# Two-layer mLSTM and RG-LRU trunk on one core: sums of weight blocks held back and spread over the layer, and block products placed away from the gates

## The chip, the cores and the metric

The kernel runs on one core of a Trainium2 chip. The metric is device time in microseconds of one execution. Before the change the median of three runs is 1538.05 us (1536.64 to 1540.25). This kernel's engines are TensorE (PE, matmuls), VectorE (DVE), ScalarE (ACT), GpSimd (POOL) and SyncE (SP). SP and POOL mostly issue DMAs here, and each engine, and each DMA-issuing queue, works its instructions off in their order.

## The reference

`x` has 256 tokens of 2048 columns, all float32. Two layers of the same kind follow each other, then a last RMS norm:

```python
def hybrid_layer(x, norm_g, w_in, ...):
    u = rms_norm(x, norm_g)
    p = u @ w_in
    qk, v, o, z_a, ig, fg, xb, z_b = jnp.split(p, SPLIT_AT, axis=-1)
    qk = jax.nn.silu(causal_dwconv(qk, qk_conv))
    ...
    h = mlstm_chunkwise(q, k, v, i_pre, log_f)
    h = h * jax.nn.sigmoid(o)
    ...                                  # head norm
    y_a = h * jax.nn.silu(z_a)
    xc = causal_dwconv(xb, lru_conv_w) + lru_conv_b
    y_b = rg_lru(xc, w_a, b_a, w_x, b_x, lam) * jax.nn.silu(z_b)
    return x + jnp.concatenate([y_a, y_b], axis=-1) @ w_out
```

`w_in` is 2048 x 12304 and `w_out` 4096 x 2048, so each layer reads some 134 MB of weights for 256 tokens. `rg_lru` has two gates, each a block-diagonal product of `xc` with a 256 x 256 block per head and a sigmoid, and then a linear recurrence over the tokens.

## The kernel before

**Tiles and stages.** A layer is worked in four groups g of 512 columns (two heads). For each group there are "in" items (o, qk, v, z, xb, zb: 512 columns of `w_in`), one "gate" item (the two gates' blocks), and for the group before four "out" items (512 columns of `w_out` each, added to x in DRAM). An item is cut into units of 1 MB of weights, a unit into two halves of 512 KB. All weights are float32 and are split for the matmuls: `prepare` copies a half to wH in a rounded format on ScalarE (L336) and subtracts it on VectorE to get wL (L186, the line of the helper `tt_`). A half of an "in" item is then twelve matmuls of 512 columns (L360): activations' high part by wH and wL, low part by wH, for two row tiles of tokens.

**The loop.** The order of halves is a list, `order_`. For each half the loop loads ahead on SP (three `raw` tiles), prepares up to three halves ahead (`AHEAD = 3`, four buffers of wH and wL), runs the matmuls, runs what follows the item (`after`), and then calls `pump`, which steps background generators by a budget. The generators do everything else: the convolutions of qk and xb, the attention, the gates' functions, the sums below. A scheduler then orders the instructions of each engine by what it expects to be ready; `order(a, b)` adds an edge that keeps a behind b on an engine, without a wait.

**Block products.** Two items of each layer, z of group 2 and o of group 3 (`PAIR`), aren't computed as such. Together they are a 2 x 2 product of blocks (tokens by input rows, input rows by the two items), and the kernel uses seven block products in place of eight. For that it needs sums of blocks:

- Sums of activations, `block_sums`: S1 to S4, made on VectorE (`sum_t`, `sums`; L186) and ScalarE (L987) from `x_s`, in pieces of 128x512.
- Sums of weights, `weight_sums`: a start transfer copies half a unit from the weights to a DRAM tile `w_d` (L1026, issued by SP), and accumulating transfers add further ones (L1028, issued by POOL). For each layer that is 8 starts and 16 accumulations of 512 KB each. The last eight accumulations wait until the products 5 and 6 have loaded what they overwrite.
- The products, `block_halves`: fourteen pairs of halves for each layer, a pair being 1 MB and only twelve matmuls (L1091 to L1093, into `ps_b`). They load from the weights or from `w_d` (L296) and are laid evenly into `order_` between the first v item and the place of z of group 2. The last one calls `z_post`.

**Other names.** `gates_gen` computes the input and forget gates (`scs`); their result goes by DMA to `nG_d` and back, broadcast, to `nb` (both on POOL's queue), from which VectorE makes `E` (L194). `swapped` transposes an evacuated item: VectorE's `blk`, four DMAs on SP to `moved` in DRAM, one back on POOL's queue to `fr`. `xcs` (L186) is the split of the convolved xb, `xc`; the gate's matmuls (L792, `ps_gt`) read it, and ScalarE's sigmoids, exponentials and square roots (L797 to L828) follow. `z_post` computes `sz` on ScalarE and `za` on VectorE and starts the product with the attention's result.

Of the kernel before, what the change touches and what calls it, by code (L numbers as in the profile page):

```python
# [9 lines left out]
F32 = mybir.dt.float32  # L10
# [19 lines left out]
BORDER = 7  # L30
BLANKS = 7


# [59 lines left out]
def tile_trunk(ctx, tc, x, xt, par, gw, gb, ws, final_g, out):  # L93
# [189 lines left out]
    def load_unit(hf):  # L283
# [4 lines left out]
        if n < 4:  # L288
            w = 512 if n == 0 else 1024
            u = blocks[item, j]  # L290
            for o in range(0, 2048, w):
                if o % 1024 == 0:
                    load_xt(n, o // 1024)
                nc.sync.dma_start(out=raw[:, o : o + w], in_=ws[u][:, o : o + w])
        elif item is None:
            nc.sync.dma_start(out=raw, in_=hf["from"])  # L296
            if "loaded" in hf:
                st[hf["loaded"]] = True
        elif hf["paired"]:
            o = 1024 * (j % 2)  # L300
            for s_ in range(2):
                u = blocks[item, 2 * s_ + j // 2]
                nc.sync.dma_start(out=raw[:, 1024 * s_ : 1024 * s_ + 1024], in_=ws[u][:, o : o + 1024])
        else:
            nc.sync.dma_start(out=raw, in_=ws[blocks[item, j]])
        if 3 <= n < 7:
# [164 lines left out]
    def swapped(tok, blk=None, back=G):  # L471
# [7 lines left out]
        for a in range(4):  # L479
            nc.sync.dma_start(out=moved[:, a].rearrange("(m j) n -> j m n", m=4), in_=blk[32 * a : 32 * a + 32])  # L480
        back.dma_start(out=fr.rearrange("p a c t i -> p a (c t i)"), in_=moved)
        return fr
# [434 lines left out]
    def out_chunk(l, g, c):  # L917
# [54 lines left out]
    def block_sums(l):  # L972
# [3 lines left out]
        def part(r, c, a, k):  # L976
            return x_.bitcast(F32)[:, 8 * c + k : 8 * c + k + 4, a, P * r : P * r + P]

        def made(i, key, terms):
            to = sums[i]  # L980
            for k in (0, 4):
                ks = slice(k, k + 4)
                two = [work.tile([P, 4, P], F32, tag=tag, name="sum_t") for tag in ("tok", "blk")]
                for a in range(2):
                    terms(two, a, k, ks)
                tt_(two[0], two[0], two[1], ALU.add)
                S.copy(out=to[:, 0, ks], in_=two[0])  # L987
                tt_(to[:, 1, ks], two[0], to.bitcast(F32)[:, 0, ks], ALU.subtract)
                yield 2.6
            st[key, l] = True  # L990

        def s1(two, a, k, ks):
            tt_(two[a], part(1, 1, a, k), part(1, 0, a, k), ALU.subtract)

        def s2(two, a, k, ks):
            stt(two[a], sums[0].bitcast(F32)[:, a, ks], -1.0, part(0, 0, a, k), ALU.mult, ALU.subtract)

        def s3(two, a, k, ks):
            tt_(two[a], part(0, 0, a, k), part(1, 0, a, k), ALU.subtract)

        def s4(two, a, k, ks):
            tt_(two[a], sums[0].bitcast(F32)[:, a, ks], part(0, 0, a, k), ALU.add)
# [13 lines left out]

    def weight_sums(l):


        def moved(to, start, r, c):  # L1020
# [11 lines left out]
        yield from moved(0, True, 0, 0)  # L1032
        yield from moved(0, False, 0, 1)
        yield from moved(1, True, 1, 1)
        yield from moved(1, False, 0, 1)
        while ("loaded", l, 5) not in st:
            yield "wait"
        yield from moved(0, False, 1, 1)
        while ("loaded", l, 6) not in st:
            yield "wait"  # L1040
        yield from moved(0, False, 1, 0)

    def block_halves(l):
# [28 lines left out]
        def end4():  # L1072
# [8 lines left out]
            bg.append(gen())  # L1081
            z_post(l, PAIR[0][1], st["res", l])

# [338 lines left out]
```

## Time and profile before

| What | Value |
|---|---|
| Runs, median (lowest to highest) | 1538.05 us (1536.64 to 1540.25) |
| Profiled execution: its time | 1541.39 us |
| Profiled execution: its span | 1539.7 us |
| PE busy | 1490.2 us, 97% |
| DVE busy | 1138.8 us, 74% |
| ACT busy | 964.4 us, 63% |
| HBM over the span | 265 GB/s |
| Mean granted TensorE clock | 0.986 |

The profile is of one execution. Group rows name line, engine, operation and tiles, then count, busy time, mean duration in ns, idle time of the engine just ahead and who ended it. A half's twelve matmuls overlap, so a row's mean duration (392 ns) isn't the time that a further one costs; that is read from how many run in a full window. A row of windows gives a stretch, its length, the five engines' busy time, the granted clock, the DMA engines' mean busy share and GB/s. Layer 0 runs until about 745 us and layer 1 from there.

### The profile page before, as it was taken

How to read it: one execution, taken by the hardware profiler on the slowest of the kernel's cores; microseconds unless marked ns; L12 is line 12 of the kernel's file. 1: busy time of each engine (PE TensorE's matmuls, PEld its weight loads, DVE VectorE, ACT ScalarE, POOL GpSimd, SP SyncE). 2: the span in 40 equal slices, each digit the busy share in tenths (PEclk: the TensorE clock that was granted, in tenths of full speed). 3: DMA queues.
4: the chain of work that ended last, by engine and by line, in shares of the span. 5: the costliest groups of instructions: out<-in, count | busy, mean ns of one | idle time of the engine just before them, and what ended most of it. 6: DMA issues, size and time to landing. Idle time of an engine off the chain costs nothing.

```text
span 1539.7 us, 18745 instructions
## 1 busy us (share of the span) xinstructions
PE 1490.2 (97%) x6782; PEld 1232.9 (80%) x6782; DVE 1138.8 (74%) x1562; ACT 964.4 (63%) x1242; POOL 112.5 (7%) x186
## 2 busy tenths in 40 slices
PE   9978879999999999999999999999999999999997
PEld 7857758888788888888888877888888888888886
DVE  5777766767776787676975999865896578767785
ACT  6545656556655685657675568655675567755675
POOL 0050100000000000000000000000000000000002
PEclk9999889999999999999999999999999999999999
DMA  9999968886977776876696575787778687678773
GB/s 337 305 266 326 276 213 250 244 266 221 286 246 253 243 225 234 254 263 221 229 334 210 190 271 170 260 241 247 264 253 280 228 256 235 239 227 265 246 261 122
DMA packets 100014, 383.44 MB, mean 249 GB/s; under 512 B 10944, under 2 KB 31440, under 8 KB 76880
## 3 DMA queue, kind: packets, MB, share of 16 engines
q1 hardware_dynamic: 83504, 327.41, 60.8%
q0 software_dynamic: 13952, 50.35, 15.6%
q10 hardware_dynamic: 2464, 4.47, 0.8%
q8 instruction: 53, 0.87, 0.2%
q14 instruction: 41, 0.34, 0.1%
HBM read 344.95 MB, written 62.41 MB: 265 GB/s over the span
## 4 chain that ended last, share of the span: by engine, by line
PE 74%; DMA 10%; DVE 5%; issue 5%; ACT 5%; SPq 1%; POOL 0%; ACTq 0%; POOLq 0%; DVEq 0%
PE acc L360 62%; DMA raw<-in_ws_dram 6%; DVE wL L186 2%; PE ps_gt L792 2%; ACT wH L336 2%; DMA moved<-blk 2%; PE acc L373 1%; DMA fr<-moved 1%; PE ps_b L1092 1%; PE ps_b L1093 1%; PE ps_b L1091 1%; DMA nb<-nG_d 1%; DVE xc L189 1%; DMA nG_d<-scs 1%; PE acc L1187 1%
## 5 line engine op out<-in xcount | busy, mean ns | idle before, releaser
L360 PE MATMUL acc<-wH,x_s 128*128 128x512 f32 x2752 | 862.0, 392 | 13.3 <-ACT wH L336 13.2
L186 DVE TENSOR_TENSOR wL<-raw,wH 128x1024 fp32r<-128x1024 f32 (+1 forms) x556 | 663.4, 1202 | 284.5 <-ACT wH L336 282.6
L336 ACT CAST wH<-raw 128x1024 fp32r<-128x1024 f32 (+1 forms) x556 | 570.2, 1037 | 390.7 <-PE acc L360 277.7
L360 PEld LDWEIGHTS acc<-wH,x_s 128*128 128x128 f32 x2752 | 520.7, 189 | 124.5 <-ACT wH L336 16.7
L360 PE MATMUL acc<-wL,x_s 128*128 128x512 f32 x1376 | 540.3, 394 | 17.3 <-DVE wL L186 17.2
L360 PEld LDWEIGHTS acc<-wL,x_s 128*128 128x128 f32 x1376 | 260.6, 189 | 78.1 <-DVE wL L186 24.4
L360 PE MATMUL acc<-wH,yaH 128*128 128x512 f32 x224 | 87.5, 391 | 0.0
L360 PE MATMUL acc<-wH,yaL 128*128 128x512 f32 x224 | 87.3, 390 | 0.0
L360 PE MATMUL acc<-wH,ybL 128*128 128x512 f32 x224 | 87.3, 390 | 0.0
L360 PE MATMUL acc<-wH,ybH 128*128 128x512 f32 x224 | 87.2, 389 | 0.0
L360 PE MATMUL acc<-wL,ybH 128*128 128x512 f32 x224 | 87.2, 389 | 0.0
L360 PE MATMUL acc<-wL,yaH 128*128 128x512 f32 x224 | 87.2, 389 | 0.0
L792 PE MATMUL ps_gt<-xcs,wH 128*128 128x256 f32 x256 | 47.3, 284 | 5.4 <-ACT gate L797 5.4
L477 DVE STREAM_TRANSPOSE blk<-tok 128x1024 f32<-128x1024 f32 x33 | 40.9, 1239 | 15.0 <-ACT tok L467 14.8
L360 PEld LDWEIGHTS acc<-wH,ybL 128*128 128x128 f32 x224 | 42.1, 188 | 9.1 <-DVE ybL L186 0.3
L360 PEld LDWEIGHTS acc<-wH,yaL 128*128 128x128 f32 x224 | 42.0, 188 | 8.9
L360 PEld LDWEIGHTS acc<-wL,ybH 128*128 128x128 f32 x224 | 42.1, 188 | 8.5
L360 PEld LDWEIGHTS acc<-wH,ybH 128*128 128x128 f32 x224 | 42.0, 188 | 8.6
L360 PEld LDWEIGHTS acc<-wH,yaH 128*128 128x128 f32 x224 | 42.1, 188 | 8.4
L360 PEld LDWEIGHTS acc<-wL,yaH 128*128 128x128 f32 x224 | 42.1, 188 | 8.2
L467 ACT ACTIVATE tok<-acc,rstd 128x512 f32<-128x512 f32 x46 | 29.2, 684 | 28.5 <-PE acc L360 27.6
L792 PEld LDWEIGHTS ps_gt<-xcs,wH 128*128 128x128 f32 x256 | 41.1, 192 | 6.5 <-ACT gate L797 5.7
(233 smaller groups left out, 1554.2 us busy)
## 6 DMA issues: line engine op xcount, KB each, us to landing
raw<-in_ws_dram SPq DMA_DIRECT2D x164, 1024.0 KB, 6.3
raw<-in_ws_dram SPq DMA_DIRECT2D x190, 512.0 KB, 6.6
fr<-moved POOLq DMA_DIRECT2D x34, 512.0 KB, 6.3
moved<-blk SPq DMA_DIRECT2D x132, 128.0 KB, 2.9
w_d<-in_ws_dram POOLq DMA_DIRECT2D x32, 512.0 KB, 10.3
raw<-w_d SPq DMA_DIRECT2D x16, 1024.0 KB, 5.0
x_d<-stage POOLq DMA_DIRECT2D x24, 512.0 KB, 6.2
w_d<-in_ws_dram SPq DMA_DIRECT2D x16, 512.0 KB, 9.1
```

The costliest lines, as they stand in the source:

```text
L186: return V.tensor_tensor(out=o, in0=a, in1=b, op=op)
L189: return V.scalar_tensor_tensor(out=o, in0=a, scalar=s, in1=b, op0=op0, op1=op1)
L336: st["wH"] = S.copy(out=H[:, o], in_=r[:, o])
L360: st["mm"] = PE.matmul(o, a_[:, kt, P * t : P * t + P], W[:, k], start=b, stop=z)
L373: PE.matmul(ps[:, ct, T * part : 2 * T], W[:, k, P * ct : P * ct + P], moving, start=first and k == 0 and part == 0, stop=last and k == 3 ...
L467: S.activation(out=by_block(tok, t), in_=acc[:, t, :].rearrange("p (c m j) -> p c m j", c=4, m=4), func=AF.Copy, scale=rstd[:, t : t + 1])
L477: V.transpose(out=blk.rearrange("p m n -> p (m n)"), in_=tok.rearrange("p m c t j -> p (m c t j)"))
L792: PE.matmul(o, W[:, ib, jl], xs[:, ib, a, :], start=j == 0 and i == 0 and W is Hv and a == 0, stop=i == 1 and W is Lv, skip_group_check=True)
L1091: PE.matmul(box["b"], aH, Hv[:, k], start=kp == 0 and k == 0, stop=False)
L1092: PE.matmul(box["b"], aH, Lv[:, k], start=False, stop=False)
L1093: PE.matmul(box["b"], aL, Hv[:, k], start=False, stop=kp == 3 and k == 1)
L1187: PE.matmul(o, yH[:, kt, tsl], Lv[:, k, cs], start=False, stop=False)
```

## The change

It touches four things.

1. **Weight sums** are one background generator for both layers, where each layer had its own; it takes four steps of `pump` per transfer (`PACE`) where it took two. A start is ordered behind the latest load of weights on SP (`st["ld"]`), an accumulation behind the latest other DMA on POOL (`st["gq"]`).
2. **Block sums** are made in pieces of 128x256, twice as many, ordered behind the latest split of weights; in layer 0 they wait for the first group's attention to be done.
3. **Block products** of layer 0 start at qk of the second group; in both layers they end six halves ahead of z's place and keep off the ten halves from each gate on. `z_post` is called at z's place and no longer with the last product.
4. **`pump`** isn't called after a half of a block product.

```diff
+PACE = 4
...
-            nc.sync.dma_start(out=raw, in_=hf["from"])
+            st["ld"] = nc.sync.dma_start(out=raw, in_=hf["from"])
...
-                G.dma_start(out=xd[c], in_=stage, accum_op=ALU.add)
+                st["gq"] = G.dma_start(out=xd[c], in_=stage, accum_op=ALU.add)
...
-            for k in (0, 4):
-                ks = slice(k, k + 4)
-                two = [work.tile([P, 4, P], F32, tag=tag, name="sum_t") for tag in ("tok", "blk")]
+            for k in (0, 2, 4, 6):
+                ks = slice(k, k + 2)
+                two = [work.tile([P, 2, P], F32, tag=tag, name="sum_t") for tag in ("tok", "blk")]
...
-                S.copy(out=to[:, 0, ks], in_=two[0])
+                order(S.copy(out=to[:, 0, ks], in_=two[0]), st["wH"])
                 tt_(to[:, 1, ks], two[0], to.bitcast(F32)[:, 0, ks], ALU.subtract)
-                yield 2.6
+                yield 1.6
...
         def s1(two, a, k, ks):
-            tt_(two[a], part(1, 1, a, k), part(1, 0, a, k), ALU.subtract)
+            order(tt_(two[a], part(1, 1, a, k), part(1, 0, a, k), ALU.subtract), st["wL"])
...
+        while l == 0 and ("hn", 0, 0) not in st:
+            yield "wait"
         yield from made(0, "S1", s1)
...
-    def weight_sums(l):
+    def weight_sums():
...
                     if start:
-                        nc.sync.dma_start(out=wd[l][to][j][:, cs], in_=src)
+                        order(nc.sync.dma_start(out=wd[l][to][j][:, cs], in_=src), st["ld"])
                     else:
-                        G.dma_start(out=wd[l][to][j][:, cs], in_=src, accum_op=ALU.add)
-                    yield "wait"
-                    yield "wait"
+                        order(G.dma_start(out=wd[l][to][j][:, cs], in_=src, accum_op=ALU.add), st["gq"])
+                    for _ in range(PACE):
+                        yield "wait"
...
-            z_post(l, PAIR[0][1], st["res", l])
...
-            beside(weight_sums(l))
+            if l == 0:
+                beside(weight_sums())
...
-        if (item[0], what) == ("in", ("v", 0)):
+        if (item[0], what) == ("in", ("v", 0) if l else ("qk", 1)) and l not in span:
             span[l] = (len(order_), None)
...
         a, b = span[l]
+        b += b % 2
+        order_[b - 1]["then"] = lambda l=l: z_post(l, PAIR[0][1], st["res", l])
+        b -= 6
         pairs = block_halves(l)
+        gates_ = [n for n, hf in enumerate(order_) if hf.get("at", (("",),))[0][0] == "gate"]
+        free = [n for n in range(a, b, 2) if not any(g <= n < g + 10 for g in gates_)]
         for i in reversed(range(len(pairs))):
-            at = a + (i + 1) * (b - a) // len(pairs)
-            at += at % 2
+            at = free[(i + 1) * (len(free) - 1) // len(pairs)]
             order_[at:at] = pairs[i]
...
+        if "then" in hf:
+            hf["then"]()
...
-        pump(1.05 if sum(g not in aside for g in bg) <= 2 else 2.6)
+        if "from" not in hf:
+            pump(1.05 if sum(g not in aside for g in bg) <= 2 else 2.6)
```

How the instructions move is decided by the scheduler, so here are three places of the engines' orders. The names w_d_118 to w_d_121 are layer 0's four tiles of weight sums, w_d_122 to w_d_125 layer 1's.

**SP, layer 0, from the loads of the first v item on.** Before:

```order
L1026 DMA w_d_118<-in_ws_dram 128x1024
L305 DMA raw<-in_ws_dram 128x2048
L1026 DMA w_d_118<-in_ws_dram 128x1024
L1026 DMA w_d_119<-in_ws_dram 128x1024
L480 DMA moved<-blk 32x4x256 x4
L303 DMA raw<-in_ws_dram 128x1024 x8
L1026 DMA w_d_119<-in_ws_dram 128x1024
L1026 DMA w_d_120<-in_ws_dram 128x1024 x2
L296 DMA raw<-in_ws_dram 128x2048
L1026 DMA w_d_121<-in_ws_dram 128x1024
L303 DMA raw<-in_ws_dram 128x1024 x2
L1026 DMA w_d_121<-in_ws_dram 128x1024
```

With the change:

```order
L306 DMA raw<-in_ws_dram 128x2048 x4
L481 DMA moved<-blk 32x4x256 x4
L304 DMA raw<-in_ws_dram 128x1024 x6
L1030 DMA w_d_118<-in_ws_dram 128x1024
L304 DMA raw<-in_ws_dram 128x1024 x4
L1030 DMA w_d_118<-in_ws_dram 128x1024
L304 DMA raw<-in_ws_dram 128x1024 x4
L1030 DMA w_d_119<-in_ws_dram 128x1024
L304 DMA raw<-in_ws_dram 128x1024 x2
L481 DMA moved<-blk 32x4x256 x4
L306 DMA raw<-in_ws_dram 128x2048
L1030 DMA w_d_119<-in_ws_dram 128x1024
```

Layer 0's starts now stand one or two weight units apart, and the first load of a block product (L296 before) isn't among these rows any more. Layer 1's eight starts followed right behind before; they now stand among the loads of layer 0's groups 2 and 3.

**POOL, layer 0, first group.** Before:

```order
L1028 DMA w_d_118<-in_ws_dram 128x1024 x2
L1028 DMA w_d_119<-in_ws_dram 128x1024
L481 DMA fr<-moved 128x1024
L570 DMA nG_d_116<-scs 8x256
L598 DMA nb<-nG_d_116 128x512
L588 COPY at_746<-scs 32x16 x4
L588 COPY at_747<-scs 32x16 x4
L1028 DMA w_d_119<-in_ws_dram 128x1024
L1028 DMA w_d_120<-in_ws_dram 128x1024 x2
L613 AFFINE_SELECT E<-E 128x128 x4
L1028 DMA w_d_121<-in_ws_dram 128x1024 x2
L1028 DMA w_d_122<-in_ws_dram 128x1024 x2
```

With the change:

```order
L482 DMA fr<-moved 128x1024
L573 DMA nG_d_116<-scs 8x256
L601 DMA nb<-nG_d_116 128x512
L591 COPY at_746<-scs 32x16 x4
L591 COPY at_747<-scs 32x16 x4
L616 AFFINE_SELECT E<-E 128x128 x4
L482 DMA fr<-moved 128x1024
L1032 DMA w_d_118<-in_ws_dram 128x1024
```

The first accumulations moved from ahead of fr, nG_d and nb to behind the second fr, and layer 1's (w_d_122 and on) out of this stage.

**VectorE, layer 1, ahead of the first group's gate.** Before, the convolution and the first half of its split:

```order
L189 SCALAR_TENSOR_TENSOR xc<-ch,pars,xc 128x255 x2
L189 SCALAR_TENSOR_TENSOR xc<-ch,pars,xc 128x254 x2
L189 SCALAR_TENSOR_TENSOR xc<-ch,pars,xc 128x253 x2
L189 SCALAR_TENSOR_TENSOR xc<-ch,pars,xc 128x255 x2
L189 SCALAR_TENSOR_TENSOR xc<-ch,pars,xc 128x254 x2
L189 SCALAR_TENSOR_TENSOR xc<-ch,pars,xc 128x253 x2
L186 TENSOR_TENSOR xcs<-xc,xcs 128x2x256
L713 BN_STATS bs<-hh 128x6 x2
L714 BN_AGGR mv<-bs 128x2
L186 TENSOR_TENSOR wL<-raw,wH 128x1024
```

With the change, a piece in which the sums stand, and further on the end of the convolution:

```order
L187 TENSOR_TENSOR wL<-raw,wH 128x1024
L187 TENSOR_TENSOR sums_7089<-sum_t,sums_7089 128x256
L187 TENSOR_TENSOR sum_t<-sums_7088,x_s 128x256 x2
L187 TENSOR_TENSOR sum_t<-sum_t,x_s 128x256 x2
L187 TENSOR_TENSOR PL<-Pt,PH 128x768
L187 TENSOR_TENSOR sum_t<-sum_t 128x256
L187 TENSOR_TENSOR wL<-raw,wH 128x1024
```

```order
L195 TENSOR_SCALAR hh<-hh,mv,sd 128x256 x4
L190 SCALAR_TENSOR_TENSOR xc<-ch,pars,xc 128x253
L190 SCALAR_TENSOR_TENSOR xc<-ch,pars,xc 128x255 x2
L190 SCALAR_TENSOR_TENSOR xc<-ch,pars,xc 128x254 x2
L190 SCALAR_TENSOR_TENSOR xc<-ch,pars,xc 128x253 x2
L187 TENSOR_TENSOR xcs<-xc,xcs 128x2x256
L187 TENSOR_TENSOR tok<-hh,za 128x4x4x32
L187 TENSOR_TENSOR xcs<-xc,xcs 128x2x256
```

Before, all of xc stood ahead of the norm of the attention's result (`bs`, `mv`); now its last seven rows stand behind the normalised `hh`, and sixteen rows of the sums stand in the stretch ahead. On PE, two halves of the next group's qk stand ahead of this gate's matmuls, which they did not before.

More of the change, by code (lines that the diff above doesn't have):

```diff
@@ L480, in swapped @@
             nc.sync.dma_start(out=moved[:, a].rearrange("(m j) n -> j m n", m=4), in_=blk[32 * a : 32 * a + 32])
-        back.dma_start(out=fr.rearrange("p a c t i -> p a (c t i)"), in_=moved)
+        i0 = back.dma_start(out=fr.rearrange("p a c t i -> p a (c t i)"), in_=moved)
+        if back is G:
+            st["gq"] = i0
         return fr
@@ L1015, in tile_trunk, with moved @@
     wd = [[[dram.tile([P, 2048], F32, name=f"w_d{l}{i}{j}") for j in range(2)] for i in range(2)] for l in range(DEPTH)]
-    def weight_sums(l):
-        def moved(to, start, r, c):
+    def weight_sums():
+        def moved(l, to, start, r, c):
             for j in range(2):
@@ L1025, in moved @@
                     if start:
-                        nc.sync.dma_start(out=wd[l][to][j][:, cs], in_=src)
+                        order(nc.sync.dma_start(out=wd[l][to][j][:, cs], in_=src), st["ld"])
                     else:
-                        G.dma_start(out=wd[l][to][j][:, cs], in_=src, accum_op=ALU.add)
-                    yield "wait"
-                    yield "wait"
[L1032 to L1041, printed above, removed]
+                        order(G.dma_start(out=wd[l][to][j][:, cs], in_=src, accum_op=ALU.add), st["gq"])
+                    for _ in range(PACE):
+                        yield "wait"
+        for l in range(DEPTH):
+            yield from moved(l, 0, True, 0, 0)
+            yield from moved(l, 0, False, 0, 1)
+            yield from moved(l, 1, True, 1, 1)
+            yield from moved(l, 1, False, 0, 1)
+            while ("loaded", l, 5) not in st:
+                yield "wait"
+            yield from moved(l, 0, False, 1, 1)
+            while ("loaded", l, 6) not in st:
+                yield "wait"
+            yield from moved(l, 0, False, 1, 0)
     def block_halves(l):
```

12 lines of the change are left out of this document (6 added, 6 removed).

## The prediction

> **What bounds the kernel now.** I read the page first: its busy rows, then the span in 40 slices (38.5 us each).
>
> ```profile
> PE 1490.2 (97%) x6782; PEld 1232.9 (80%) x6782; DVE 1138.8 (74%) x1562; ACT 964.4 (63%) x1242; POOL 112.5 (7%) x186
> ...
> PE   9978879999999999999999999999999999999997
> ...
> PEclk9999889999999999999999999999999999999999
> DMA  9999968886977776876696575787778687678773
> ```
>
> TensorE is the bound, and the 97% is an average over one bad stage and many full ones: PE falls below 9 only in slices 3 to 6, where DMA shows 9 and the granted clock 8. So I cut the span into windows (columns: PE, PEld, DVE, ACT and POOL busy, granted clock, DMA share, GB/s).
>
> ```profile
> 60.00:220.00 160.00, 129.80 (x556) 104.54 (x555) 116.23 (x193) 84.66 (x113) 31.93 (x36) 0.90 0.93 273
> 220.00:240.00 20.00, 20.00 (x82) 16.33 (x82) 15.45 (x19) 11.98 (x14) 1.53 (x5) 0.91 0.78 257
> 240.00:400.00 160.00, 160.00 (x742) 133.65 (x741) 117.50 (x157) 97.83 (x120) 9.18 (x12) 1.00 0.80 246
> 400.00:740.00 340.00, 337.44 (x1572) 280.89 (x1571) 248.58 (x326) 220.47 (x273) 17.47 (x33) 1.00 0.76 246
> 540.00:560.00 20.00, 18.77 (x95) 15.50 (x94) 18.95 (x30) 15.38 (x21) 1.71 (x2) 1.00 0.81 207
> 780.00:800.00 20.00, 20.00 (x90) 16.57 (x89) 14.81 (x17) 17.29 (x34) 2.58 (x4) 1.00 0.99 332
> 920.00:940.00 20.00, 20.00 (x121) 17.87 (x120) 19.74 (x51) 14.69 (x20) 0.11 (x1) 1.00 0.52 184
> 940.00:960.00 20.00, 17.20 (x67) 13.27 (x67) 18.11 (x21) 19.91 (x31) 0.53 (x1) 0.91 0.62 206
> 1200.00:1220.00 20.00, 20.00 (x90) 16.57 (x89) 9.80 (x8) 9.45 (x10) 0.00 (x0) 1.00 0.64 247
> 1280.00:1300.00 20.00, 18.77 (x83) 15.08 (x82) 18.58 (x32) 17.15 (x21) 1.73 (x2) 1.00 0.84 223
> ```
>
> The undisturbed window 1200:1220 prices a 512-column matmul: 20/90 = 0.222 us, so a half of twelve is 2.67 us. With that price each window's matmuls become the time they would need. For 60:220 the groups are:
>
> ```profile
> L360 PE MATMUL acc<-wH,x_s 128*128 128x512 f32 x297 | 98.2, 408 | 11.1 <-ACT wH L336 11.1
> L360 PE MATMUL acc<-wL,x_s 128*128 128x512 f32 x149 | 61.9, 415 | 12.3 <-DVE wL L186 12.3
> L792 PE MATMUL ps_gt<-xcs,wH 128*128 128x256 f32 x32 | 6.9, 318 | 5.4 <-ACT gate L797 5.4
> L1091 PE MATMUL ps_b<-wH,x_s 128*128 128x512 f32 x12 | 4.7, 389 | 0.0
> ```
>
> With two more ps_b groups of 12, that is 482 matmuls of 512 columns: 107.1 us. The 48 gate matmuls (32 with wH, 16 with wL) are 5.6 us at 0.117 (4.20/36, a row of the chain below), the small attention ones some 4 us. So 117 us of work took 160: **43 us lost**, and with 18.6 us of work in 220:240 about 44.9. The same count finds 5.1 us lost in 940:960 (67 x 0.222 = 14.9, after the first gate of layer 1) and about 2 each in 540:560 and 1280:1300, at the gates of group 2.
>
> What the stage 60:220 is short of, the DMA view of that window says, beside the next stage's two load rows:
>
> ```profile
> q1 hardware_dynamic: 9251, 32.59, 56.0%
> q0 software_dynamic: 3072, 11.02, 37.2%
> ...
> raw<-in_ws_dram SPq DMA_DIRECT2D x24, 512.0 KB, 11.9
> raw<-in_ws_dram SPq DMA_DIRECT2D x10, 1024.0 KB, 8.9
> w_d<-in_ws_dram POOLq DMA_DIRECT2D x15, 512.0 KB, 10.5
> w_d<-in_ws_dram SPq DMA_DIRECT2D x13, 512.0 KB, 9.6
> ```
>
> ```profile
> raw<-in_ws_dram SPq DMA_DIRECT2D x19, 1024.0 KB, 7.0
> raw<-in_ws_dram SPq DMA_DIRECT2D x16, 512.0 KB, 5.6
> ```
>
> Loads of weights land in 11.9 us there against 5.6 afterwards, and 28 of the 48 transfers for weight sums, of both layers, are in these 160 us. Who waits, in the same window:
>
> ```profile
> DVE wL L186 <- ACT wH L336: 28.4, 8, 11.6
> ...
> ACT wH L336 <- DMA raw<-in_ws_dram: 27.0, 7, 8.3
> ```
>
> ScalarE waits for the weights, VectorE for ScalarE, PE for both.
>
> **The change, term by term.** (1) *The sum transfers held back.* The added orders put no wait on a queue, they only say who stands ahead. The SP and POOL orders show layer 0's transfers spread over some 30 weight loads and layer 1's moved to groups 2 and 3. Prices from the window: q0 took 37.2% of 160 = 59.5 us for 15 accumulating transfers, 4 fr and two half-size nb: about 3 us each. q1 took 89.6 us for 32.59 MB, 2.75 us a MB, so a 0.5 MB start costs 1.4. The 28 transfers cost 15 x 3 + 13 x 1.4 = 63 us of the 149 us that the engines were busy. Of the changed order some 4 accumulations and 6 starts fall beside the same matmuls: 20 us; two block loads of 1 MB leave too, 5 us. What stays is 149 - 63 + 20 - 5 = 101 us of transfers for 117 us of PE: no longer the bound, but at 0.86 not idle. I leave 4 us of the loss to late landings.
>
> (2) *POOL's queue.* nG_d no longer stands behind three accumulations. The chain shows the path of both layers:
>
> ```profile
> 72.16 14.21 issue
> 86.38 5.88 DMA nG_d<-scs
> 92.55 5.71 DMA nb<-nG_d
> 373.65 4.20 PE ps_gt L792 x36
> 876.47 3.03 DMA nG_d<-scs
> 879.78 4.65 DMA nb<-nG_d
> ```
>
> The 14.2 us ahead of 86.38 go. VectorE still stands at E, with the split of weights queued behind it, until nb lands; layer 1 has that wait without other traffic and loses about 1.3 us. I leave 2.
>
> (3) *Halved sums.* VectorE's prices:
>
> ```profile
> L186 DVE TENSOR_TENSOR wL<-raw,wH 128x1024 fp32r<-128x1024 f32 x540 | 652.4, 1218 | 280.5 <-ACT wH L336 278.6
> L186 DVE TENSOR_TENSOR sum_t<-sum_t 128x512 f32<-128x512 f32 x16 | 10.9, 683 | 0.2
> L186 DVE TENSOR_TENSOR Pt<-ps_S,Pt 128x256 f32<-128x256 f32 x16 | 6.6, 410 | 0.0
> ```
>
> 72 instructions of 0.683 become 144 of about 0.41: 49.2 us become 59, +10 over both layers. VectorE's idle time (280.5 us ahead of wL alone) hides it, except where it is already the one waited for.
>
> (4) *The gates.* That is the case ahead of the gate of group 0 and of group 2. Product halves no longer step the background work, so the convolution xc comes out later, in layer 0 among the sums, in layer 1 behind them; both xcs rows then stand right before the gate that needs them. In layer 1, between the wL ahead of Pt and the second xcs, the new order has 6 wL (7.3 us), 16 rows of the sums (6.6), twelve xc and some 35 small rows. The twelve xc are one row of the timeline:
>
> ```profile
> 923.69 4.81 DVE L189 SCALAR_TENSOR_TENSOR xc<-ch,pars,xc 128x255 f32<-128x255 f32 x12
> ```
>
> In 920:940 VectorE did 51 instructions in 19.74 us, 0.39 each with the large ones among them; at about a third of a microsecond the 35 are 11 us. Together 30 us, beside which PE has 60 matmuls and 12 of 258 columns: 14.7 us. The excess is 15. The split runs ahead by three halves less its own 1.2 us, 7 us. **Layer 1's first gate loses 8, and 1 by the clock: 9**, in place of the 5.1 in 940:960. Those had another cause:
>
> ```profile
> 949.13 0.49 PE L1091 MATMUL ps_b<-wH,x_s 128*128 128x512 f32 x1 [2.33 <-ACT wH L336]
> ```
>
> a block product right behind the gate while ScalarE was at the gate's functions; the change takes that product away. The same count gives 33 us of VectorE to 21 of PE at layer 0's first gate, excess 12, **6 lost** with the clock. At the gates of group 2, where z_post's two za now stand as well, it gives 22.5 to 11.3, excess 11; the order before counts 29 to 19, excess 10, and loses 2. So 3.5, or +1.5 each. Bounds for each gate: nothing (all covered) and the whole excess.
>
> The windows' rows tell that a wait costs more than itself: 940:960 has 2.8 us without a matmul and loses 5.1, at a clock of 0.91. The Trainium skill (TensorE: Matmul & The Clock Gate, "What's actually happening") has the clock halved after an idle window of about 3.4 us, until as long a busy one; estimated from that, each of four long waits costs up to 1.7 us more, and the sum would be some 5 us worse. The trace agrees with its direction.
>
> (5) *Layer 1's transfers in layer 0's groups 2 and 3*: 8 starts and 8 accumulations, 35 us of DMA time beside about 160 us of PE. On 0.76 (400:740) that is 0.98 at the peak if nothing else gives; some of the 0.76 is accumulation that moves earlier. PE was busy 337.44 of 340 there. I take 1 us lost, between 0 and 6. The Trainium skill (DMA: Bandwidth & Descriptors, "Issuing engines are not separate DMA queues") has all queues share the same 16 engines, so a transfer moved is a transfer paid later; the two queues' shares in 60:220 (56.0% and 37.2%, together full) agree.
>
> (6) *Layer 0's products from the second group on*: 14 loads beside about 300 us of PE, not 410. A pair brings 1 MB for 2.67 us of PE, 2.75 us of DMA. With four ordinary loads between pairs the mean is below one. Nothing.
>
> **The sum**, against the profiled execution (1541.39, span 1539.7): layer 0's stage 44.9 becomes 6 + 2 + 4 = 12, so -32.9; layer 1's first gate 9 - 5.1 = +4; the gates of group 2 +3; layer 1's transfers +1. Together -25: 1516.5. That execution is 3.3 us above the median of the runs, 1538.05; so **1513**.
>
> **The rivals.** *A: the look-ahead covers the gates.* The split may be four halves ahead where I count three, and small rows may overlap more. Then layer 0 loses 6, the gates nothing: -38.9 - 5.1 - 4 + 1 = -47: 1491. For it: over the whole span VectorE is busy 74%. Against it: 540:560 lost 2 at an excess of 10.
>
> *B: DMA stays the bound.* Matmuls that come faster ask for loads faster, and 0.86 is a mean: a load behind a start and two accumulations lands as late as before. If layer 0 keeps 28 of its 44.9, the sum is -16.9 + 4 + 3 + 1 = -9: 1529. Against it: 780:800 had a share of 0.99 and lost nothing.
>
> *C: slower.* One mechanism: VectorE at the four gates without cover. If the split isn't ahead when those stretches begin, because landings or E held it just before, the excess 15 + 12 + 11 + 11 = 49 is lost whole, with 2.3 of clock at each (5.1 lost less 2.8 idle in 940:960) 58 in place of 9: +49, against -38.9 + 1: +11, 1549. It decides once the cover is below about 2.7 us a gate; the 8 us between 10 counted and 2 lost in 540:560 speak against it.
>
> *D: no change*, B and a part of C together. That transfers really leave the stage isn't in doubt: both queues' orders show it.
>
> **How the numbers follow.** Forecast 0.58, A 0.17, B 0.17, C 0.05, D 0.03. The forecast's own range is 1505 to 1522; to leave out 2 in 10 I reach towards A and B: 1498 to 1530. This kernel's runs differ by about 0.2%, 3 us, which is what a measurement can tell. Faster 0.92 (forecast, A, B), same 0.03, slower 0.05.
>
> **What will show it.** DMA share in 60:220 near 0.85, landings of 512 KB loads 6 to 8 us, PE busy there above 150; no w_d of layer 1 before about 350 us. PE waiting at ps_gt on xcs at the first gate of both layers, some 6 and 9 us; if those waits are missing, (4) is wrong and A holds. If raw still lands in 11 us, (1) is wrong. PE waits behind raw<-w_d would be a mechanism that I haven't priced.

## The result and the profile after

The changed kernel takes 1522.68 us (median of five runs, 1519.83 to 1527.95), the kernel before 1536.7 us beside it. The ratio is 0.9907 with a 95% interval of 0.9882 to 0.9932: faster by some 14 us, where 25 were forecast. The time lies in the forecast's range (1498 to 1530) and just outside its own narrower one (1505 to 1522). The profiled execution is the slowest of the five (1527.95 us, span 1526.2), 13.5 us of span less than before's.

The page's busy rows and slices of the changed kernel:

```profile
PE 1489.4 (98%) x6782; PEld 1229.3 (81%) x6782; DVE 1140.2 (75%) x1634; ACT 966.2 (63%) x1258; POOL 107.5 (7%) x186
...
PE   9999989999999999999999998999999999999997
...
PEclk9999999999999999999999999999999999999999
DMA  9779787897879998976785674978778688677773
```

The hole in slices 3 to 6 is closed, and the clock's 8s with it. What is left are two 8s, in the sixth slice (191 to 229 us) and the 25th (916 to 954). The DMA row has a run of 9s from 458 to 572 us now, where layer 1's transfers went. Stretches of the prediction's table, and some more (columns: PE, PEld, DVE, ACT and POOL busy, granted clock, DMA share, GB/s):

```profile
60.00:220.00 160.00, 154.96 (x707) 126.59 (x706) 139.30 (x243) 102.47 (x137) 18.11 (x33) 1.00 0.81 257
220.00:240.00 20.00, 15.96 (x60) 12.64 (x59) 12.13 (x11) 11.76 (x14) 0.00 (x0) 0.83 0.77 263
...
520.00:580.00 60.00, 57.45 (x267) 47.29 (x266) 46.21 (x62) 41.27 (x55) 6.13 (x9) 0.97 0.94 278
580.00:700.00 120.00, 118.47 (x544) 98.23 (x542) 80.39 (x118) 71.78 (x87) 8.27 (x13) 0.99 0.81 260
700.00:860.00 160.00, 160.00 (x742) 133.20 (x741) 124.81 (x164) 102.86 (x147) 10.83 (x22) 1.00 0.72 245
860.00:980.00 120.00, 112.86 (x515) 91.69 (x514) 105.89 (x174) 85.52 (x115) 8.52 (x17) 0.99 0.69 225
```

In 60:220 PE works off 707 matmuls where it did 556, at full clock. In 220:240 it has 60 where it had 82. From the DMA view of 60:220 in the changed kernel (tiles, queue, count, size, median us from issue to landing):

```profile
raw<-in_ws_dram SPq DMA_DIRECT2D x24, 512.0 KB, 6.2
...
w_d<-in_ws_dram POOLq DMA_DIRECT2D x7, 512.0 KB, 14.1
```

Loads of 512 KB land in 6.2 us (11.9 before), while 7 accumulations of 15 are left in this stretch.

To compare places I use the prediction's count: a stretch's length less its matmuls at 0.222 us for 512 columns, 0.117 for 256 (0.118 for 258, 0.062 for 128, from the spacing of their starts), counted window by window of 20 us, as the price was. What is left over is what PE lost there, in us of the profiled executions:

| Stretch, us | What lies there | Before | After | Change | Predicted |
|---|---|---|---|---|---|
| 60 to 260 | layer 0's stage and first gate | 44.4 | 15.4 | -29.0 | -32.9 |
| 520 to 580, 1260 to 1340 | gates of group 2 | 5.0 | 9.3 | +4.3 | +3 |
| 860 to 980 | layer 1's first gate | 7.2 | 12.1 | +4.9 | +4 |
| 400 to 520, 580 to 700 | layer 1's transfers, beside other work | 2.9 | 6.8 | +3.9 | +1 |
| 260 to 400, 700 to 860, 1100 to 1180 | nothing priced | 0.8 | 5.9 | +5.1 | 0 |

Together -10.8; some 3 us more lie at the start, at the end and in the price of a matmul. So every priced row has its sign. The stage gave 4 us less than forecast, and small losses elsewhere took 10 us more.

One of them can be followed from row to row. Around 220:240, POOL's timeline, then ScalarE's, then PE's, each of the changed kernel:

```profile
187.09 0.59 POOL L601 DMA_DIRECT2D nb<-nG_d  x1 [50.08 <-issue]
...
206.60 0.56 POOL L482 DMA_DIRECT2D fr<-moved  x1 [6.06 <-DMA moved<-blk]
207.16 2.59 POOL L1032 DMA_DIRECT2D w_d<-in_ws_dram  x3
```

```profile
220.28 2.00 ACT L337 CAST wH<-raw 128x1024 fp32r<-128x1024 f32 x2 [6.17 <-DMA raw<-in_ws_dram]
```

```profile
226.41 0.80 PE L361 MATMUL acc<-wH,x_s 128*128 128x512 f32 x1 [4.04 <-ACT wH L337]
227.00 0.63 PE L1096 MATMUL ps_b<-wL,x_s 128*128 128x512 f32 x1
```

POOL stands 50 us at nb (a wait whose releaser the profile doesn't name) and then at `fr`, and lets three accumulations go within 2.6 us. The loads that SP issues beside them land late:

```profile
DMA to landing us min/median/max: 5.1/9.7/14.9
```

That is the row for `raw` in 200:230. ScalarE waits 6.2 us for one of them and 3.0 for the next, PE stands for 4.0 us, and its next matmuls start 0.43 us apart instead of 0.23, at a granted clock of 0.51 in 226:232. The accumulations are spread over the program's steps, but POOL's queue gathers them again.

### The profile page after: what moved, and what is told of

Same layout as the page of the kernel before. It is cut to its first block, busy times and chain, and to the rows that moved or that the text cites. A ratio compares the mean times of both kernels' runs of the same rounds, so it can differ in the third digit from the quotient of the medians.

```text
span 1526.2 us, 18815 instructions
## 1 busy us (share of the span) xinstructions
PE 1489.4 (98%) x6782; PEld 1229.3 (81%) x6782; DVE 1140.2 (75%) x1634; ACT 966.2 (63%) x1258; POOL 107.5 (7%) x186
## 3 DMA queue, kind: packets, MB, share of 16 engines
q0 software_dynamic: 13952, 50.35, 15.4%
## 4 chain that ended last, share of the span: by engine, by line
PE 66%; DMA 12%; DVE 10%; issue 8%; ACT 3%; SPq 0%; POOL 0%; DVEq 0%; ACTq 0%; POOLq 0%
PE acc L361 54%; DMA raw<-in_ws_dram 8%; DVE wL L187 4%; PE ps_gt L795 2%; ACT wH L337 2%; PE acc L374 1%; DMA nb<-nG_d 1%; PE ps_b L1097 1%; PE ps_b L1096 1%; PE ps_b L1095 1%; DMA fr<-moved 1%; DVE xc L190 1%; PE acc L1193 1%; PE acc L1191 1%; PE acc L1192 1%
## 5 line engine op out<-in xcount | busy, mean ns | idle before, releaser
L482 POOL DMA_DIRECT2D fr<-moved x34 | 19.0, 560 | 466.6 <-DMA moved<-blk 335.7
L190 DVE SCALAR_TENSOR_TENSOR qc<-ch,pars,qc 128x255 f32<-128x255 f32 (+2 forms) x96 | 41.4, 478 | 5.0 <-ACT qc L450 4.7
## 6 DMA issues: line engine op xcount, KB each, us to landing
w_d<-in_ws_dram POOLq DMA_DIRECT2D x32, 512.0 KB, 12.1
```

The costliest lines, as they stand in the source:

```text
L190: return V.scalar_tensor_tensor(out=o, in0=a, scalar=s, in1=b, op0=op0, op1=op1)
L482: i0 = back.dma_start(out=fr.rearrange("p a c t i -> p a (c t i)"), in_=moved)
```

## The experiments

Each kernel was timed beside the kernel before (medians of 1538.4 to 1538.7 us there). "Lost" is the count above.

| Run | Kernel | Median, us | Ratio to before (95%) |
|---|---|---|---|
| e1 | before, held-back transfers alone | 1519.31 | 0.9878 (0.986 to 0.9897) |
| e2 | change without them | 1549.9 | 1.0073 (1.0058 to 1.0087) |
| e3 | change, stepping after product halves too | 1516.36 | 0.9855 (0.984 to 0.9869) |
| e4 | change, layer 1's transfers later | 1519.71 | 0.9883 (0.987 to 0.9896) |
| e5 | e3 and e4 together | 1514.91 | 0.9848 (0.9834 to 0.9862) |
| e6 | change, no accumulations | 1512.24 | 0.9829 (0.9812 to 0.9845) |
| e7 | e1, layer 1's transfers later | 1513.86 | 0.9841 (0.9822 to 0.986) |
| e8 | change, whole sums of x | 1537.53 | 1.0001 (0.9989 to 1.0012) |
| e9 | e8, no accumulations | 1519.79 | 0.9882 (0.986 to 0.9903) |
| e10 | before, no accumulations | 1507.55 | 0.9798 (0.9782 to 0.9814) |
| e11 | change, halved sums without their order | 1527.85 | 0.9921 (0.9903 to 0.9939) |
| e12 | e1, layer 1's transfers ten steps apart | 1509.32 | 0.9809 (0.979 to 0.9827) |

### e1 and e2: which part carries the gain

e1 is the kernel before with part 1 of the diff and nothing else. e2 is the changed kernel with `weight_sums` as before:

```diff
-                        order(nc.sync.dma_start(out=wd[l][to][j][:, cs], in_=src), st["ld"])
+                        nc.sync.dma_start(out=wd[l][to][j][:, cs], in_=src)
...
-                    for _ in range(PACE):
-                        yield "wait"
+                    yield "wait"
+                    yield "wait"
```

> The kernel before with the first part alone: the transfers for the weight sums are one sequence over both layers, each four steps apart, a start behind the last weight load, an accumulation behind the last transfer on POOL. Block products, block sums and the stepping of the background work stay as before. Theory (the gain is the transfers' alone, and the other parts cost VectorE's lateness at four gates and late landings, together some 15 us): layer 0's stage loses some 12 instead of 43 us, the gates lose what they lost before, layer 1's transfers in layer 0's later groups cost 6: 1537 - 31 + 6 = 1512, faster than the changed kernel by about 10. Rival (the other parts are needed: with the two block products and the undivided sums still in that stage, its loads land late again): PE busy in 60:220 stays under 145, and the time is 1525 or more.

> The changed kernel with the transfers for the weight sums as before (two steps apart, no order, a sequence for each layer); everything else of the change stays. Theory (the transfers were the bound of 60:220): that stage keeps about 38 of its 43 us of loss, a DMA share above 0.9 and weight loads that land in some 11 us; the gates lose some 10 more than before: 1537 - 5 + 10 = 1542. Rival (the block products and sums were what crowded the stage): 60:220 gains 15 us or more without the first part, and the time is below 1530.

The first part alone takes 19 us off, and the intervals leave open whether the changed kernel is any slower than that (medians 1519 and 1523). The rest alone is 11 us slower than before, and 8 above its expectation. The window 60:220 of e1, then of e2:

```profile
60.00:220.00 160.00, 154.06 (x702) 125.75 (x701) 141.96 (x228) 106.89 (x139) 32.03 (x33) 1.00 0.84 267
```

```profile
60.00:220.00 160.00, 144.31 (x630) 117.33 (x629) 127.83 (x226) 92.78 (x125) 22.33 (x40) 0.95 0.94 284
```

So the gain is the held-back transfers': e1 has the changed kernel's 60:220 with the sums and products as before. The rival for e2 had half a point: the rest alone does bring 74 matmuls more into that stretch (loss 25 instead of 43), and loses it again later (13 us in 1100:1180 alone; by what, isn't followed here).

e1 missed its 1512 by 7. It loses 9 us in 400:520, at one load. POOL's timeline of e1, then ScalarE's:

```profile
453.72 0.87 POOL L935 DMA_DIRECT2D x_d<-stage  x1 [3.85 <-ACT stage L934]
454.27 2.04 POOL L1030 DMA_DIRECT2D w_d<-in_ws_dram  x2
471.01 0.88 POOL L935 DMA_DIRECT2D x_d<-stage  x1 [14.70 <-ACT stage L934]
471.57 2.02 POOL L1030 DMA_DIRECT2D w_d<-in_ws_dram  x2
```

```profile
488.53 1.99 ACT L337 CAST wH<-raw 128x1024 fp32r<-128x1024 f32 x2 [9.76 <-DMA raw<-in_ws_dram]
```

Four accumulations of layer 1 and two to `x_d` go within 18 us, and ScalarE then waits 9.8 us for a load. e7 and e12 take these four away from there.

### e3, e4 and e5: the gates and layer 1's transfers

e3 steps after product halves again, e4 holds layer 1's sequence until layer 0's last gate is done, e5 has both:

```diff
-        if "from" not in hf:
-            pump(1.05 if sum(g not in aside for g in bg) <= 2 else 2.6)
+        pump(1.05 if sum(g not in aside for g in bg) <= 2 else 2.6)
```

```diff
         for l in range(DEPTH):
+            while l and ("lru", 0, NG - 1) not in st:
+                yield "wait"
             yield from moved(l, 0, True, 0, 0)
```

> The changed kernel, but the background work is stepped after the halves of block products too, as before. Theory (the convolution xc comes late on VectorE since product halves don't step it, and that costs about 4 us at layer 1's first gate and 5 at the gates of group 2): those come back, 1523 - 9 = 1514. Rival (what is lost there and elsewhere are late landings, behind accumulations that POOL lets go in groups): no gain, 1520 to 1526.

> The changed kernel, but layer 1's transfers for the weight sums begin only when layer 0's last gate is done, so that they lie in layer 1's first half instead of layer 0's groups 2 and 3. Theory (they cost 6 us in 500:660, where accumulations to x_d stand beside them): layer 0's groups 2 and 3 lose nothing but the gate, 1523 - 6 = 1517, with a DMA share in 740:920 up from 0.71 to about 0.8 and no loss there. Rival (16 transfers cost the same wherever they stand beside full PE): 1520 to 1526, with 6 us more lost between 740 and 960.

> The changed kernel with both mended: the background work is stepped after product halves too, and layer 1's transfers begin when layer 0's last gate is done. Theory (two losses with separate causes, VectorE's lateness at the gates and late landings in layer 0's groups 2 and 3): both gains add up, 1516 - 3 = 1513. Rival (one loss, seen twice: a wait that goes at one place comes back at the next): 1516 to 1520, no better than either alone.

e3's windows at layer 0's gate of group 2 and at layer 1's first gate, to be read against the changed kernel's above:

```profile
520.00:580.00 60.00, 59.73 (x286) 49.88 (x285) 44.54 (x58) 43.56 (x59) 6.95 (x10) 1.00 0.90 294
...
860.00:980.00 120.00, 118.09 (x549) 97.57 (x550) 114.21 (x181) 91.15 (x121) 14.77 (x17) 1.00 0.74 244
```

With the stepping back, 860:980 has 549 matmuls instead of 515 and loses 3.9 instead of 12.1, the other gate 0.8 instead of 5.0. 12 us come back at two gates, 6 in the time; in this execution 5 more are lost in 260:520. So the missing steps are what those two gates lost by. Layer 1's gate of group 2 is another case: 1260:1340 keeps 4.2 of its 4.3 us in e3. e4's windows:

```profile
580.00:700.00 120.00, 120.00 (x573) 100.83 (x572) 80.53 (x116) 74.93 (x94) 6.45 (x12) 1.00 0.76 243
700.00:860.00 160.00, 158.26 (x712) 129.05 (x711) 124.77 (x170) 98.14 (x138) 15.18 (x27) 1.00 0.81 274
```

Layer 0's 4.5 us of 580:700 go, and 700:860 loses 4.4 instead of 0.8. By windows of 20 us, 2.0 of these lie in 760:780, ahead of layer 1's first accumulation (776 us), where ScalarE has just waited 2.6 us for a `fr`; and 1.1 lie where VectorE waits for nb, a loss that the changed kernel has too, in 860:880 (1.6). By the medians 3 us are won, between theory and rival, but the interval overlaps the changed kernel's, so that e4 is faster at all isn't settled. e5 has 1514.91 us, 1.5 below e3; its interval overlaps e3's, so that the two gains add up isn't settled.

### e6, e9 and e10: without accumulations

e6, e9 and e10 leave the accumulating transfers out (the weight sums then hold their first block alone):

```diff
-                        order(G.dma_start(out=wd[l][to][j][:, cs], in_=src, accum_op=ALU.add), st["gq"])
+                        pass
```

> The changed kernel without the accumulating transfers into w_d (the weight sums then hold only their first block, so the outputs are wrong; every other instruction stays). Theory (the losses that are left outside the gates are weight loads that land late behind accumulations that POOL lets go in groups of two to four): the losses in 220:240 (6.7), 640:660 (3.3) and 1100:1180 (2.8) go, the gates' stay, no weight load waits over 3 us: 1523 - 11 = 1512. Rival (loads land late for lack of a raw buffer while VectorE or ScalarE is at something else; the accumulations only happen to stand there): 1518 or more, with the loss in 220:240 still there.

> The kernel before without the accumulating transfers into w_d (outputs wrong), its other transfers at the front as before. Theory (the accumulations cost most of the 43 us in 60:220, by themselves and by what stands behind them on POOL): 1538 - 35 = 1503, below the changed kernel without them, since the rest of the change costs about 8 us at the gates. Rival (the early starts and the block products of that stage cost as much): 1518 or more.

ScalarE's waits for weights over the whole run, in the changed kernel and in e6 (us in total, times, longest us):

```profile
ACT wH L337 <- DMA raw<-in_ws_dram: 95.4, 48, 6.2
```

```profile
ACT wH L337 <- DMA raw<-in_ws_dram: 25.9, 20, 3.1
```

The loss in 220:260 falls from 7.3 to 2.2 us, 580:700 from 4.5 to 0.8, 1100:1180 from 3.3 to nothing; the gates keep theirs (11.2 in 860:980). So accumulations, and the late loads beside them, cost the changed kernel 10 us, as expected (1512), and the rival for e6 falls. The kernel before gains three times as much without them, 31 us, and its first stage is nearly full with the starts still at the front:

```profile
60.00:220.00 160.00, 151.61 (x684) 124.60 (x683) 139.55 (x226) 105.53 (x138) 24.81 (x26) 0.97 0.77 265
```

Accumulations were most of that stage's load (43 us lost become 13). Of the 13 that stay, 9.5 lie in 60:140, beside the starts at the front; e6, which holds the starts back, loses 0.7 there. And without accumulations the changed kernel is some 5 us slower than the kernel before (0.9829 against 0.9798; the intervals just touch), so the rest of the change costs something there too.

### e8, e9 and e11: the sums of x

e8 takes part 2 of the change back: its sums are in pieces of 512 columns, without the order behind the split, and they don't wait for the first group's attention either. (The expectation of e8 below says that this wait stays; the kernel that ran doesn't have it.) e11 has the halved sums without the order, but with the wait; e9 is e8 without accumulations. Of e8's edit:

```diff
-            for k in (0, 2, 4, 6):
-                ks = slice(k, k + 2)
+            for k in (0, 4):
+                ks = slice(k, k + 4)
...
-                yield 1.6
+                yield 2.6
...
-        while l == 0 and ("hn", 0, 0) not in st:
-            yield "wait"
```

> The changed kernel with the sums of x in pieces of 512 columns, as before, without an order behind the split of weights (layer 0's still wait for group 0's hn). Theory (10 us more of VectorE for the halved pieces, hidden by its idle time): within 4 us of the changed kernel, 1519 to 1527. Rival (the larger pieces stand in the way of the split on VectorE): 1530 or more.

> The changed kernel with whole sums of x (the run with pieces of 512 columns) and without the accumulating transfers into w_d, so the weight sums hold only their first block and the outputs are wrong. Theory (whole sums cost 15 us because a step of theirs takes more of the stepping's budget and puts off the accumulations, nine instead of six of which then stand in 260:400, with loads up to 9 us late): without accumulations the size of the pieces doesn't matter, 1510 to 1516, as the changed kernel without them (1512). Rival (the large pieces, or their place ahead of the split, hold VectorE): 1522 or more.

> The changed kernel with the halved sums of x, but no order behind the split of weights for them. Theory (what counts of that part is how it spends the stepping's budget, which stays): within 4 us of the changed kernel, 1519 to 1527. Rival (the order keeps the sums from standing ahead of the split of weights): 1530 or more.

This was the surprise: with part 2 taken back, the whole gain is gone (1537.53, ratio 1.0001). VectorE's work on `sum_t` in 60:120, in e8 and then in the changed kernel, shows that layer 0's first sums move as well:

```profile
60.00:120.00 60.00, 13.02 (x20) 1.00 0.78 246
```

```profile
60.00:120.00 60.00, 0.00 (x0) 1.00 0.81 265
```

In the changed kernel, as in e11, they run in 120:180. The accumulations between 260 and 400 us in e8, then in the changed kernel:

```profile
w_d<-in_ws_dram POOLq DMA_DIRECT2D x9, 512.0 KB, 14.1
```

```profile
w_d<-in_ws_dram POOLq DMA_DIRECT2D x6, 512.0 KB, 12.9
```

Nine instead of six stand there, the loss of that stretch is 12.2 instead of 1.8 (and of 580:700 11.6 instead of 4.5), and ScalarE's longest wait for a load is 9.4 us. By the code, a piece that costs 2.6 overdraws a budget of 1.05 so far that the next call steps nothing, the transfers neither, and a piece of 1.6, begun at a full budget, doesn't. If putting off accumulations were all, e9 would equal e6. It is 7.6 us slower, between its two expectations. Two windows of e9, then of e6:

```profile
140.00:220.00 80.00, 71.86 (x336) 58.13 (x335) 66.60 (x106) 57.06 (x76) 2.82 (x9) 1.00 0.63 214
...
520.00:580.00 60.00, 54.09 (x250) 44.02 (x249) 43.67 (x53) 39.69 (x55) 2.49 (x5) 0.97 0.70 215
```

```profile
140.00:220.00 80.00, 77.51 (x360) 63.65 (x359) 70.68 (x104) 60.16 (x82) 2.76 (x8) 1.00 0.71 248
...
520.00:580.00 60.00, 57.30 (x265) 46.85 (x264) 44.41 (x48) 41.92 (x57) 1.76 (x4) 1.00 0.72 251
```

About half of the 15 us hang on the accumulations, then, and the other half is lost without any, mostly in the stretches of layer 0's gates of group 0 and 2. By which of the three edits (size, order or wait) either half comes stays open. e11 has the order taken away alone: 1527.85 us, just above its own theory and below the rival, and at 0.9921 its interval overlaps the changed kernel's (0.9882 to 0.9932). The order is worth between nothing and some 7 us. In e11's profile 140:220 loses 12.0 us (5.9 in the changed kernel), so an equal loss there appears with the order gone alone. Size and wait weren't run apart. And e1 has the sums as e8 has them, yet keeps its 19 us: part 2 is needed only beside the other two parts, the block products' places and the missing steps.

### e7 and e12: what layer 1's transfers cost

Both are e1 with another place for layer 1's sequence: e7 as in e4, e12 with a wider spacing.

```diff
-                    for _ in range(PACE):
+                    for _ in range(10 if l else PACE):
```

> The kernel before with the first part alone, and layer 1's transfers begun when layer 0's last gate is done. Theory (the kernel with the first part alone loses 8.4 us in 400:520 to one weight load that lands late beside four of layer 1's accumulations): that goes, 1519 - 8 = 1511, the fastest so far. Rival (that stall is the two block products in a row there): it stays, 1517 to 1520.

> The kernel before with the first part alone, layer 1's transfers ten steps apart instead of four, so that they reach from layer 0's group 2 into layer 1's first half, and their accumulations stand alone on POOL. Theory (what layer 1's transfers cost is the group of two to four accumulations, not their number): the 8 us of 400:520 go, and the 5 us that they cost in 700:860 when held back to layer 1 don't come: 1509. Rival (they cost the same wherever they are): 1514 to 1519.

e7 (1513.86 us, 1511 expected) loses 0.4 us in 400:520 where e1 lost 9.1, but 6.2 in 700:860 instead of 0.7. Of these, 1.8 lie in 760:780, as in e4, and 3.1 in 840:860, where VectorE stands at E until nb lands:

```profile
856.69 1.01 DVE L195 TENSOR_SCALAR E<-nb,at 128x256 f32<-128x256 f32 x4 [4.63 <-DMA nb<-nG_d]
```

e1 has the same wait, 2.5 us long, and loses 1.4 by it in 860:880. So what came back in e7 isn't a late load behind a group: POOL lets four accumulations go at 774.47, ScalarE waits 5.6 us for a load at 793.84, and PE loses 0.7 in 780:820. e12 loses 0.4 in 400:520 and 2.1 in 700:860. Its windows of these stretches, and two rows of its POOL timeline:

```profile
400.00:520.00 120.00, 120.00 (x541) 99.51 (x540) 86.08 (x120) 71.91 (x82) 5.11 (x11) 1.00 0.82 267
...
700.00:860.00 160.00, 159.19 (x719) 131.23 (x718) 128.00 (x166) 100.68 (x138) 13.35 (x27) 1.00 0.76 256
```

```profile
520.30 1.17 POOL L1030 DMA_DIRECT2D w_d<-in_ws_dram  x1
...
537.25 0.88 POOL L1030 DMA_DIRECT2D w_d<-in_ws_dram  x1
```

The same transfers, further apart and nearly all of layer 1's one at a time (pairs go at 770.7 and 1125.2 us): 10 us less than e1 and 13 less than the changed kernel. e12 has the lowest median of the kernels here that compute everything, 1509.32 us, as its expectation had it, with sums, products and stepping as before the change; e7's interval just touches its own, and that of the kernel before without accumulations (e10) overlaps it. Spacing and place aren't taken apart by it: where e1's four stand (454 to 472 us), e12 has no accumulation at all.

## Why the prediction was right or wrong

**Term 1, transfers held back: right.** DMA share 0.81 (0.85 forecast), 512 KB loads at 6.2 us (6 to 8), PE busy 154.96 us (over 150), no transfer of layer 1 early on; and e1 against e2 shows that the gain is this part's. The 4 us left for late landings were too few: 220:240, behind one group of three accumulations, loses 5 more than before, and in e6 it doesn't.

**Term 2, POOL's queue: the row was misread.** "The 14.2 us ahead of 86.38 go": they didn't. POOL's rows for nG_d before, then with the change:

```profile
86.38 0.53 POOL L570 DMA_DIRECT2D nG_d<-scs  x1 [14.22 <-DVE scs L193]
```

```profile
81.16 0.55 POOL L573 DMA_DIRECT2D nG_d<-scs  x1 [15.03 <-DVE scs L194]
```

In both, nG_d waits for VectorE's `scs`, not for accumulations ahead of it in the queue; without any accumulation (e10) it still waits 14.5 us and goes at 80.62. What came earlier is `scs`, by 5 us, since VectorE no longer stands 4.5 us at a late wH; and nG_d lands sooner, so that nb goes at 83.41 instead of 92.55. 60:140 loses 2.2 instead of 18.9. No run takes this gain apart from term 1; that POOL's queue held nG_d isn't shown.

**Term 3, halved sums hidden: too narrow.** The sums' rows add up to 58.8 us of VectorE instead of 48.6, as said, and e8, with whole pieces, isn't faster. But the term asked only what the halves cost VectorE, and they are worth 15 us together with their order and their wait (e8). What a step takes from the budget, and where the sums stand, wasn't in the working.

**Term 4, the gates: cause right at two of four, form wrong.** e3 shows the missing steps to be the cause at layer 1's first gate and at layer 0's gate of group 2. Layer 1's first gate lost 4.9 more than before (4 forecast), the two of group 2 4.3 (3). The sign that I named, PE waiting at `ps_gt` on xcs for 6 and 9 us, is missing: those waits are 0.2 and 1.8 us. PE's waits in 860:980 of the changed kernel:

```profile
PE acc L361 <- DVE wL L187: 3.7, 4, 1.7
PE ps_gt L795 <- DVE xcs L187: 1.8, 1, 1.8
```

VectorE's lateness shows at wL, ahead of the gate and behind it, since both go through one queue. So the named sign, by which A was to hold, misled: the gates did cost. For layer 0's first gate I had 6 us by the same count. 140:220 loses 5.9 in all, and e3 changes that by 0.6: there the missing steps weren't the cause, nor at layer 1's gate of group 2, and that 5.9 and 6 agree is luck.

**Term 5, layer 1's transfers: the step that failed.** "I take 1 us lost, between 0 and 6." In the changed kernel the stretches beside them lose 3.9 more, and in e1 the same transfers cost 10 us against e12. The working went by the mean share of the DMA engines (0.76 and what is added). Of the 3.9 us, 3.4 lie in 640:660, behind these rows of POOL, then of ScalarE, in the changed kernel:

```profile
613.92 1.20 POOL L1032 DMA_DIRECT2D w_d<-in_ws_dram  x1
...
625.34 1.21 POOL L1032 DMA_DIRECT2D w_d<-in_ws_dram  x1
```

```profile
638.88 1.99 ACT L337 CAST wH<-raw 128x1024 fp32r<-128x1024 f32 x2 [5.73 <-DMA raw<-in_ws_dram]
```

A load lands late though the mean share is below one, and without accumulations (e6) 640:660 loses 0.1. So accumulations are the cause; that they must go in groups isn't: these went one by one, each right behind an accumulation to `x_d`. In 220:240 and in e1's 400:520 they went in groups, and there an accumulation ordered behind `fr` or `x_d` waits with it and the next ones catch up. How much of the loss is the grouping, no run takes apart.

**Not priced:** 5.1 us in three stretches. Of the 2.7 in 1100:1180, some 2 lie behind a group of three accumulations at 1143.66 (the rest ahead of it), but e4 has such a group too (at 1134.04) and loses nothing. A group makes a late load possible; whether PE feels it may depend on how far the split is ahead just then. That isn't settled further.

**The rivals.** B (DMA stays the bound, 1529) falls by 60:220. A (the gates are covered, 1491) falls by e3, and nothing came near its time; without any accumulation the kernel before needs 1507.55. C and D fall by the result.

## What to carry to other kernels

A mean share of the DMA engines says what a stage can bear, not when a load lands: look up what goes beside it and which transfers an in-order queue lets go together, since spreading them in the program doesn't spread them behind a queue that stands. A change of four parts should be timed part by part: here one part held all the gain, and a wider spacing of that part alone (1509) beat the whole (1523). Where background work is stepped by a budget, the code lets the size of one generator's step set the time of all others; how much that was worth here isn't shown apart.

## What the runs showed of the hardware

PE's clock fell after waits much shorter than I had reckoned with. Two places in PE's timeline of the changed kernel:

```profile
639.97 0.50 PE L361 MATMUL acc<-wH,x_s 128*128 128x512 f32 x1 [0.77 <-ACT wH L337]
641.23 0.60 PE L361 MATMUL acc<-wL,x_s 128*128 128x512 f32 x1 [0.76 <-DVE wL L187]
641.64 1.05 PE L361 MATMUL acc<-wH,x_s 128*128 128x512 f32 x2
```

```profile
1299.87 0.50 PE L361 MATMUL acc<-wH,x_s 128*128 128x512 f32 x1 [0.93 <-ACT wH L337]
1301.33 0.50 PE L361 MATMUL acc<-wL,x_s 128*128 128x512 f32 x1 [0.96 <-DVE wL L187]
1301.67 0.62 PE L361 MATMUL acc<-wH,x_s 128*128 128x512 f32 x2
```

At 640 two waits of 0.77 us are followed by matmuls at 0.43 us each (1.05 for two, overlapping) until 645, and the granted clock is 0.57 in 641:645 (1.00 in 639:641 and in 645:648): 1.5 us of waiting lose 3.4. At 1300 two longer waits are followed by matmuls at full pace, at a clock of 1.00. The waits come in such pairs because a late wH (behind a late load at 640, behind the gate's functions on ScalarE at 1300) makes wL late too, one split later. The Trainium skill (TensorE: Matmul & The Clock Gate, "Why this matters for your kernels") asks for no idle gaps over some 3 us between bursts. The first place shows the clock halved after two gaps of under 0.8, so here the measurement decides. The Trainium skill's free-running window (the same page, "What's actually happening") might explain why the second pair got away; no run here moves a pair against such a window, so this isn't shown.
